# Low pieces of weights: from a GpSimd subtraction to a ScalarE copy and an adding transfer

## The chip, the cores and the metric

The kernel runs on one core of a Trainium2 chip. The metric is the device time of one execution in microseconds, shown as the median of several runs of the same program. The times of the profile are microseconds from the first instruction of one profiled execution. PE is TensorE (its weight loads are PEld), DVE is VectorE, ACT is ScalarE, POOL is GpSimd and SP is the queue that issues most loads.

## The reference, cut to what matters

The program is a two-layer backbone over 256 tokens of 2048 channels: an even layer (a convolution and a state-space layer in parallel), an odd layer (a gated MLP over chunks), each followed by a convolutional feed-forward part. What matters here is that nearly all of the work is products of activations with large float32 weights:

```python
proj = hn @ w_in                       # even mixer, 2048 x 3584
out = concat([y_conv, y_ssm]) @ w_out  # 2048 x 2048
z = gelu(hn @ w_in)                    # odd mixer, 2048 x 4096
...
z = hn @ w_in                          # feed-forward, 2048 x 8192, twice
return (a * silu(g)) @ w_out           # 4096 x 2048, twice
```

Beside them stand the modulation vectors, `silu(c) @ ada_w[layer]`, which read 2048 x 12288 weights for each layer.

## The kernel before

A product of float32 precision is made from products of a rounded type, float32r: both operands are cut into a high piece (the value rounded to float32r) and a low piece (the value less its high piece), and `mm3` adds three products, high by high (L137), high by low weights (L138) and low by high weights (L139), into one bank of PSUM.

`groups` goes through the weights in slabs of [128, 2048] float32 (1 MB): it loads a slab into a buffer `raw` (four of them, L157, on SP's queue), and for each half of it calls `split`, which fills a pair of buffers `hi` and `lo` (three of each, 128 x 1024); then come the 12 products of that half (two k tiles, two blocks of 128 tokens, three products of 512 columns each). In what follows one such half, with its 12 products, is called a split. There are 568 of them.

In `split` ACT writes `hi` as a copy of the half of `raw` (L130), and then POOL or DVE writes `lo` as `raw` less `hi` (L132 and L133). Which of them does it, `pool_every` sets: POOL takes every fourth or third split, or none, in parts of the even layer, and every second one from the end of the even mixer on (`PE5`, L1331). From there on splits come in pairs, one whose `lo` DVE makes and one whose `lo` POOL makes. A split can only begin when its buffers are free, and as there are three, that is when PE has finished the split three places ahead of it.

The order of the instructions on each engine comes from a scheduler that follows the order of the program and the priorities: loads and splits are written under `high_priority` (L156 and L161), `AHEAD2` places early. Each engine and each queue works strictly in its order.

Beside this, DVE does the 3x3 convolutions of the feed-forward part (`conv9`, L1249), the sums of the modulation vectors of the second layer (`ada_items_v`: slabs `rawa` of 512 KB, two buffers, loaded at L242 and multiplied and added into `adacc` at L244), the residual adds and the low pieces of the activations. PE does part of the modulation products of the first layer (L202), transposes (L1233, L390) and the rest. POOL's only other DMAs are five small loads at the start and while the state-space layer is built, among them `bc_in` (L617).

Of the kernel before, what the change touches and what calls it, by code (L numbers as in the profile page):

```python
# [8 lines left out]
F32 = mybir.dt.float32  # L9
# [49 lines left out]
class Builder:  # L59
# [68 lines left out]
    def split(self, hi, lo, raw):  # L128
        nc = self.nc
        nc.scalar.activation(hi, raw, AF.Copy)  # L130
        self.split_n += 1
        eng = nc.gpsimd if self.split_n % self.pool_every == 0 else nc.vector  # L132
        eng.tensor_sub(lo, raw, hi.bitcast(F32))  # L133
# [7 lines left out]
    def groups(self, wap, gs, toks, qs, ada=(0.0, 0.0), rate=None, crate=0.0, width=2, order=None, hold=0,  # L141
               hfs=(0, 1)):
        """ps[g][t] = x_t @ W[:, 512 g : 512 g + 512]; qs: (slab, first k tile of x)."""
# [81 lines left out]
    def ada_items_v(self, l, v):  # L225
        """the same with the products of the slabs on the vector engine, summed over partitions at the end."""
# [41 lines left out]
    def ada_pump(self, n, k=0):  # L268
        """n slabs' worth of the queue of products on the tensor engine (k = 0) or the vector engine (k = 1)."""
        q = self.ada_q[k]  # L270
        self.ada_credit[k] = min(self.ada_credit[k] + n, max(n, 4.0))
        while q and self.ada_credit[k] >= q[0][0]:
            c, f = q[0]
            q.pop(0)
            f()
            self.ada_credit[k] -= c
# [10 lines left out]
    def gate_row(self, l, v):  # L287
        """row form of a gate vector on every partition."""
        self.ada_until(self.ada_row, (l, v))
        row = self.hp.tile([128, D], F32, name="grow", tag="grow")  # L290
        for j in range(4):
            self.nc.sync.dma_start(row[:, 512 * j:512 * j + 512],
                                   self.ada_row[l, v][j:j + 1].to_broadcast([128, 512]))
        return row

    def mod_vecs(self, l, which, s=0):
        """(norm_g * (1 + scale), shift) with channels on partitions."""
# [28 lines left out]
    def ssq_rms(self, ssq, n, tag):  # L326
        """ssq [128, t, parts] -> 1/rms per token; the columns' chains are interleaved."""
# [38 lines left out]
    def norm_chunk(self, k0, nk, rows, r, gs, sh, xh, xl):  # L366
        """nk k tiles from k0 of the modulated rows, transposed and split."""
# [16 lines left out]
    def transposed(self, z, b):  # L384
        """PSUM [128 ch, 2, 256 tok]: channel tiles b, b + 1 of the token-major pair z."""
# [69 lines left out]
    def ada0_items(self, k0, nk):  # L455
        """shift and scale of the first mixer for both streams, nk k tiles from k0: quadrants hold the
        scale's even and odd k tiles, then the shift's."""
# [126 lines left out]
    def s5_powers(self):  # L584
        """ab^e (e = 1 .. 3) and f ab^k (k = 0 .. 4), channels (re, im)."""
# [24 lines left out]
    def s5_compact(self, T, p):  # L610
        """closures: powers of ab times C f and B for four pairs, both directions."""
# [25 lines left out]
    def s5_input(self, u):  # L637
        """u [128 tok (i, chunk), 4 (ctx, ctx, lat, lat), 512] -> X[(i, 32 ch), pair, chunk]."""
# [14 lines left out]
    def s5_tables(self, T, d, t, k):  # L653
        """cos and sin of the angle per chunk for four pairs."""
# [13 lines left out]
    def s5_group(self, T, d, sp):  # L668
        """closures for four pairs of state groups in one direction."""
# [138 lines left out]
    def s5_gelu(self, T):  # L808
        """closure: gelu of 128 channels of the readout, channels on partitions."""
# [16 lines left out]
    def s5_output(self, mh, ml):  # L826
        """gate of the readout, split into the last four k tiles."""
# [15 lines left out]
    def conv31(self, cts):  # L843
        """closures: 31 taps over some z tiles."""
# [15 lines left out]
    def conv31_pe(self, cts):  # L860
        """closures: the same by products with diagonal matrices of the taps."""
# [221 lines left out]
    # LayerNorm over channels on partitions.  # L1083
    def ln_items(self, zpp):
# [9 lines left out]
        def total(ps):  # L1094
            """the quadrants' sums (each on 32 partitions) added up, on every partition."""
# [125 lines left out]
    def conv9(self, z, ct, dst):  # L1221
        """closures: transposes of two 128-channel tiles of z and their 3x3 grid convolutions into dst."""
# [35 lines left out]
    def ffn(self, l, h, ssq, ada, ada_out):  # L1258
# [4 lines left out]
        with self.tc.tile_pool(name=f"fp{l}", bufs=1) as fp:  # L1263
# [7 lines left out]
            def half(g, gi):  # L1271
                """closures after the product of column group g (gi: pair)."""
# [92 lines left out]
def tile_w(w):  # L1365
    """[K, N] -> [N/512, K/512, 128, 4 * 512]"""
    K, N = w.shape
    return w.reshape(K // 512, 4, 128, N // 512, 512).transpose(3, 0, 2, 1, 4).reshape(N // 512, K // 512, 128, 2048)


def chan(v):
    """[..., n * 128] -> [128, ..., n]"""
# [4 lines left out]
def layout(i):  # L1377
# [31 lines left out]
    def state(v):  # L1409
        """[2, 32, 64, 16] -> [4 T, (2 g, 64), 2 d, 4 q, 16]"""  # L1410
# [34 lines left out]
```

## Time and profile before

| | us |
|---|---|
| median of 3 runs | 2123.08 |
| lowest and highest of them | 2120.01, 2129.16 |
| profiled execution (its span, first to last instruction) | 2123.7 |
| PE busy | 1960.5 |
| DVE busy | 1697.2 |
| ACT busy | 984.5 |
| POOL busy | 794.8 |

The profile gives the profiled execution's time as its span; nothing beside it is listed. A busy engine is one that has an instruction under way; matmuls overlap, so PE can show as busy while it is not at its fastest. The chain of work that ended last is followed back from the last instruction through whatever released each step. A stretch of the timeline shows starts and durations, so that an end is the sum of the two.

### The profile page before, as it was taken

What the parts mean: (1) busy time and instruction counts of PE and PEld (TensorE: products, weight loads), DVE (VectorE), ACT (ScalarE), POOL (GpSimd) and SP (SyncE); (2) the same over time, 40 slices, a digit from 0 to 9 for tenths busy, and PEclk for the clock granted to TensorE, in tenths of its full rate; (3) what the DMA queues carried; (4) which work ended last, traced back from release to release, by engine and by line L of the source; (5) the groups of instructions that cost most, each with busy time, mean ns of one, the idle gap of its engine ahead of it and who ended that gap; (6) DMA issues with size and microseconds to landing.
All of it is one profiled execution on the core that took longest, in us unless ns stands there. A gap on an engine that the chain in (4) does not pass through costs nothing.

```text
span 2123.7 us, 26033 instructions
## 1 busy us (share of the span) xinstructions
PE 1960.5 (92%) x9384; PEld 1500.1 (71%) x9384; DVE 1697.2 (80%) x2806; ACT 984.5 (46%) x1407; POOL 794.8 (37%) x384
## 2 busy tenths in 40 slices
PE   5999999899899999999999789899899989999997
PEld 2566566686677776778777567777677867888886
DVE  5469998977778997789999776976789997368874
ACT  3354344663455543345454354343455543355553
POOL 4312203511033444445445244443433443444443
PEclk8999999899999999999999899999999999999999
DMA  9985766444866677787667777767765576555552
GB/s 380 394 345 220 265 251 258 169 174 185 311 250 255 237 274 260 280 291 249 223 235 274 265 256 284 269 252 290 265 238 211 195 246 239 181 192 184 182 203 110
DMA packets 91645, 522.47 MB, mean 246 GB/s; under 512 B 11334, under 2 KB 11590, under 8 KB 41974
## 3 DMA queue, kind: packets, MB, share of 16 engines
q1 hardware_dynamic: 88684, 517.09, 66.3%
q10 hardware_dynamic: 2448, 2.57, 0.4%
q8 instruction: 73, 1.20, 0.2%
q0 software_dynamic: 384, 1.16, 0.1%
q14 instruction: 56, 0.46, 0.1%
HBM read 518.65 MB, written 2.13 MB: 245 GB/s over the span
## 4 chain that ended last, share of the span: by engine, by line
PE 30%; DVE 21%; issue 7%; DMA 7%; POOL 3%; ACT 1%; SPq 0%; ACTq 0%; DVEq 0%; POOLq 0%
PE mm L137 10%; PE mm L138 9%; PE mm L139 9%; DVE adacc L244 7%; DMA rawa<-in_ada_w 6%; DVE lo L133 5%; POOL lo L133 3%; DVE ca L1249 3%; DVE cg L1249 3%; PE tp L1233 1%; DVE ca L1299 1%; DVE al L1301 1%; ACT hi L130 0%; DVE h L411 0%; DVE wk L410 0%
## 5 line engine op out<-in xcount | busy, mean ns | idle before, releaser
L133 POOL TENSOR_TENSOR lo<-raw,hi 128x1024 fp32r<-128x1024 f32 x258 | 693.7, 2689 | 1201.0 <-ACT hi L130 1115.9
L130 ACT ACTIVATE hi<-raw 128x1024 fp32r<-128x1024 f32 x568 | 599.1, 1059 | 773.6 <-PE mm L139 612.0
L138 PE MATMUL mm<-lo,xh 128*128 128x512 f32 x1632 | 649.8, 398 | 41.9 <-DVE lo L133 41.0
L137 PE MATMUL mm<-hi,xh 128*128 128x512 f32 x1632 | 656.9, 404 | 3.5 <-DVE acc L993 1.9
L139 PE MATMUL mm<-hi,xl 128*128 128x512 f32 x1632 | 646.2, 397 | 3.0 <-DVE xl L1136 1.7
L133 DVE TENSOR_TENSOR lo<-raw,hi 128x1024 fp32r<-128x1024 f32 x310 | 422.4, 1365 | 154.9 <-ACT hi L130 154.4
L244 DVE SCALAR_TENSOR_TENSOR adacc<-rawa,cst,adacc 128x1024 f32<-128x1024 f32 x192 | 336.1, 1757 | 101.2 <-DMA rawa<-in_ada_w 98.1
L138 PEld LDWEIGHTS mm<-lo,xh 128*128 128x128 f32 x1632 | 311.5, 191 | 115.9 <-DVE lo L133 53.3
L137 PEld LDWEIGHTS mm<-hi,xh 128*128 128x128 f32 x1632 | 311.0, 191 | 108.1 <-issue 31.7
L139 PEld LDWEIGHTS mm<-hi,xl 128*128 128x128 f32 x1632 | 310.5, 190 | 72.2 <-DVE xl L1136 3.3
L138 PE MATMUL mm<-lo,ah 128*128 128x512 f32 x640 | 258.8, 404 | 13.8 <-DVE lo L133 13.1
L137 PE MATMUL mm<-hi,ah 128*128 128x512 f32 x640 | 257.8, 403 | 0.0
L139 PE MATMUL mm<-hi,al 128*128 128x512 f32 x640 | 257.0, 402 | 0.0
L1249 DVE SCALAR_TENSOR_TENSOR ca<-tp,fcw,ca 128x189 f32<-128x189 f32 (+2 forms) x512 | 179.6, 418 | 12.6 <-ACT ca L1236 12.6
L1249 DVE SCALAR_TENSOR_TENSOR cg<-tp,fcw,cg 128x189 f32<-128x189 f32 (+2 forms) x512 | 179.9, 418 | 9.1 <-ACT cg L1236 9.1
L138 PEld LDWEIGHTS mm<-lo,ah 128*128 128x128 f32 x640 | 122.7, 192 | 48.1 <-DVE lo L133 17.2
L137 PEld LDWEIGHTS mm<-hi,ah 128*128 128x128 f32 x640 | 122.7, 192 | 32.1 <-issue 2.5
L139 PEld LDWEIGHTS mm<-hi,al 128*128 128x128 f32 x640 | 122.8, 192 | 31.4 <-issue 2.5
L856 DVE SCALAR_TENSOR_TENSOR zc<-zpad,ecw,zc 128x256 f32<-128x256 f32 x300 | 139.1, 530 | 0.0
L202 PE MATMUL ad<-raw,cst 128*32 128x512 f32 x512 | 79.4, 621 | 3.6 <-DVE wk L210 2.7
L390 PE MATMUL tp<-ident,wk 128*128 128x128 f32 x184 | 34.3, 314 | 29.9 <-DVE wk L376 16.7
L411 DVE TENSOR_TENSOR h<-h,wk 128x512 f32<-128x512 f32 x56 | 57.4, 1034 | 1.1
(279 smaller groups left out, 1519.0 us busy)
## 6 DMA issues: line engine op xcount, KB each, us to landing
raw<-in_f_w_in SPq DMA_DIRECT2D x128, 1024.0 KB, 4.8
rawa<-in_ada_w SPq DMA_DIRECT2D x192, 512.0 KB, 5.2
raw<-in_ada_w SPq DMA_DIRECT2D x84, 1024.0 KB, 6.1
raw<-in_f_w_out SPq DMA_DIRECT2D x64, 1024.0 KB, 4.8
raw<-in_o_w_in SPq DMA_DIRECT2D x32, 1024.0 KB, 6.8
raw<-in_e_w_in SPq DMA_DIRECT2D x28, 1024.0 KB, 7.0
raw<-in_e_w_out SPq DMA_DIRECT2D x16, 1024.0 KB, 6.9
raw<-in_o_w_out SPq DMA_DIRECT2D x16, 1024.0 KB, 6.9
```

The lines of the kernel that those rows point to most:

```text
L130: nc.scalar.activation(hi, raw, AF.Copy)
L133: eng.tensor_sub(lo, raw, hi.bitcast(F32))
L137: nc.tensor.matmul(ps, xh, wh, start=first, stop=False)
L138: nc.tensor.matmul(ps, xh, wl, start=False, stop=False)
L139: nc.tensor.matmul(ps, xl, wh, start=False, stop=last)
L202: nc.tensor.matmul(st["ps"][32 * j:32 * j + 32, :], self.cst[:, kt], raw[:, 512 * j:512 * j + 512], start=kt == 0, stop=kt == KT - 1, tile ...
L244: nc.vector.scalar_tensor_tensor(a, raw, self.cst[:, kt, 0:1], a, op0=OP.mult, op1=OP.add)
L390: self.nc.tensor.transpose(tp[:, a * 256 + t * 128:a * 256 + t * 128 + 128], z[t][:, c0:c0 + 128], self.ident)
L411: nc.vector.tensor_add(h[:, t, c], h[:, t, c], m)
L856: nc.vector.scalar_tensor_tensor(o, src, w, o, op0=OP.mult, op1=OP.add)
L1233: nc.tensor.transpose(tp[:, a * 256 + t * 128:a * 256 + t * 128 + 128], z[t][:, c0 + 128 * a:c0 + 128 * a + 128], self.ident)
L1249: nc.vector.scalar_tensor_tensor(oo, s[:, y0 + dy:y1 + dy, x0 + dx:x1 + dx], w, oo, op0=OP.mult, op1=OP.add)
```

## The change

For the splits that were POOL's, `lo` is made in two steps: ACT writes the negated, rounded half of `raw` into `lo`, and a DMA issued from POOL's queue adds `raw` to it in place, from SBUF to SBUF. DVE's splits stay as they are. All else in the diff is comments and blank lines that went, which moves the lines that follow by five.

```diff
     def split(self, hi, lo, raw):
         nc = self.nc
         nc.scalar.activation(hi, raw, AF.Copy)
         self.split_n += 1
-        eng = nc.gpsimd if self.split_n % self.pool_every == 0 else nc.vector
-        eng.tensor_sub(lo, raw, hi.bitcast(F32))
+        if self.split_n % self.pool_every:
+            nc.vector.tensor_sub(lo, raw, hi.bitcast(F32))
+        else:
+            nc.scalar.activation(lo, raw, AF.Copy, scale=-1.0)
+            nc.gpsimd.dma_start(lo.bitcast(F32), raw, accum_op=OP.add)
```

The scheduler's order on ACT, in the second feed-forward part, where two column groups of its first product are copied out of PSUM (`z`). Two slabs stand here; of each, the first half is DVE's and the second was POOL's. Before:

```order
L130 ACTIVATE hi_15089<-raw_15087 128x1024
L130 ACTIVATE hi_15114<-raw_15087 128x1024
L1278 ACTIVATE z_15079<-mm_14895 128x512
L130 ACTIVATE hi_15138<-raw_15136 128x1024
L1278 ACTIVATE z_15081<-mm_14896 128x512
L130 ACTIVATE hi_15160<-raw_15136 128x1024
```

And with the change (L132 is the copy to `hi`, L137 the negated copy to `lo`):

```order
L132 ACTIVATE hi_15315<-raw_15313 128x1024
L137 ACTIVATE lo_15341<-raw_15313 128x1024
L132 ACTIVATE hi_15340<-raw_15313 128x1024
L1283 ACTIVATE z_15305<-mm_15117 128x512
L132 ACTIVATE hi_15365<-raw_15363 128x1024
L1283 ACTIVATE z_15307<-mm_15118 128x512
L137 ACTIVATE lo_15388<-raw_15363 128x1024
L132 ACTIVATE hi_15387<-raw_15363 128x1024
```

The negated copy has come in as one more instruction for every slab, and it stands ahead of the copy to `hi` of its own split, although the program writes it behind.

POOL's order from the end of the even layer to the end of the program, before:

```order
L133 TENSOR_TENSOR lo<-raw,hi 128x1024 x39
L232 MEMSET adacc 128x2048
L133 TENSOR_TENSOR lo<-raw,hi 128x1024 x30
L232 MEMSET adacc 128x2048
L133 TENSOR_TENSOR lo<-raw,hi 128x1024 x28
```

And with the change:

```order
L138 DMA lo<-raw 128x1024 x39
L237 MEMSET adacc 128x2048
L138 DMA lo<-raw 128x1024 x30
L237 MEMSET adacc 128x2048
L138 DMA lo<-raw 128x1024 x29
```

Each subtraction has become an issue of a DMA in the same place; the clearing of `adacc` stays between them, one place later in the last case.

## Rows read from the trace of the kernel before

**Rows 1.** The page, busy time of each engine, share of the span, instructions.

```profile
PE 1960.5 (92%) x9384; PEld 1500.1 (71%) x9384; DVE 1697.2 (80%) x2806; ACT 984.5 (46%) x1407; POOL 794.8 (37%) x384
```

**Rows 2.** The page, chain that ended last: shares by engine, then by line.

```profile
PE 30%; DVE 21%; issue 7%; DMA 7%; POOL 3%; ACT 1%; SPq 0%; ACTq 0%; DVEq 0%; POOLq 0%
PE mm L137 10%; PE mm L138 9%; PE mm L139 9%; DVE adacc L244 7%; DMA rawa<-in_ada_w 6%; DVE lo L133 5%; POOL lo L133 3%; DVE ca L1249 3%; DVE cg L1249 3%; PE tp L1233 1%; DVE ca L1299 1%; DVE al L1301 1%; ACT hi L130 0%; DVE h L411 0%; DVE wk L410 0%
```

**Rows 3.** Three stretches, all instructions.

```profile
core 0: us, PE busy (x) PEld busy (x) DVE busy (x) ACT busy (x) POOL busy (x), PEclk, DMA share, GB/s
0.00:100.00 100.00, 75.23 (x372) 40.15 (x376) 51.84 (x180) 36.94 (x63) 43.83 (x64) 0.91 0.96 385
600.00:1600.00 1000.00, 922.35 (x4037) 727.18 (x4037) 830.14 (x1100) 449.32 (x566) 426.19 (x157) 0.97 0.73 262
1600.00:2123.00 523.00, 499.01 (x2216) 403.97 (x2215) 397.36 (x715) 253.44 (x316) 214.66 (x86) 0.99 0.54 193
```

**Rows 4.** The same stretches, low pieces (L133) alone: DVE, POOL, clock, DMA.

```profile
600.00:1600.00 1000.00, 218.67 (x152) 417.21 (x152) 0.97 0.73 262
1600.00:2123.00 523.00, 110.89 (x87) 214.66 (x86) 0.99 0.54 193
```

**Rows 5.** Timeline of PE, 1920 to 1927: start, duration, instruction.

```profile
1920.35 0.39 PE L138 MATMUL mm<-lo,xh 128*128 128x512 f32 x1
1920.58 0.39 PE L139 MATMUL mm<-hi,xl 128*128 128x512 f32 x1
1920.81 0.60 PE L1233 MATMUL tp<-ident,z 128*128 128x128 f32 x4
...
1926.73 0.39 PE L137 MATMUL mm<-hi,xh 128*128 128x512 f32 x1
1926.96 0.39 PE L138 MATMUL mm<-lo,xh 128*128 128x512 f32 x1
```

**Rows 6.** Timelines of ACT and POOL, the split that belongs to these.

```profile
1921.01 1.06 ACT L130 ACTIVATE hi<-raw 128x1024 fp32r<-128x1024 f32 x1 [1.61 <-PE mm L139]
1922.14 2.41 POOL L133 TENSOR_TENSOR lo<-raw,hi 128x1024 fp32r<-128x1024 f32 x1 [2.97 <-ACT hi L130]
```

**Rows 7.** Who waited for whom: us in total, times, longest.

```profile
POOL lo L133 <- ACT hi L130: 1115.9, 244, 36.8
ACT hi L130 <- PE mm L139: 612.0, 369, 7.2
DVE adacc L244 <- DMA rawa<-in_ada_w: 98.1, 52, 5.6
PE mm L138 <- DVE lo L133: 54.0, 34, 2.9
```

**Rows 8.** The page, groups: busy us, mean ns | idle before, releaser.

```profile
L133 POOL TENSOR_TENSOR lo<-raw,hi 128x1024 fp32r<-128x1024 f32 x258 | 693.7, 2689 | 1201.0 <-ACT hi L130 1115.9
L133 DVE TENSOR_TENSOR lo<-raw,hi 128x1024 fp32r<-128x1024 f32 x310 | 422.4, 1365 | 154.9 <-ACT hi L130 154.4
L244 DVE SCALAR_TENSOR_TENSOR adacc<-rawa,cst,adacc 128x1024 f32<-128x1024 f32 x192 | 336.1, 1757 | 101.2 <-DMA rawa<-in_ada_w 98.1
```

**Rows 9.** The same instructions by line or tile: ns least/median/most.

```profile
L130 ACT ACTIVATE hi<-raw x568: 1040/1061/1079, 35.7 to 2102.7; 128x1024 fp32r<-128x1024 f32 x190
L133 DVE TENSOR_TENSOR lo<-raw,hi x310: 1199/1218/3415, 38.4 to 2101.1; 128x1024 fp32r<-128x1024 f32 x155
L244 DVE SCALAR_TENSOR_TENSOR adacc<-rawa,cst,adacc x192: 1216/1282/3449, 547.0 to 1767.7; 128x1024 f32<-128x1024 f32 x192
```

**Rows 10.** Line L617, POOL's loads of 256 KB: issue in ns, then landing.

```profile
L617 POOL DMA_DIRECT2D bc_in<-in_s_bc x4: 536/578/585, 2.5 to 374.4; - x4
...
DMA to landing us min/median/max: 3.0/6.6/8.2
```

**Rows 11.** Tile rawa, SP's loads of 512 KB: issue in ns, then landing.

```profile
L242 SPq DMA_DIRECT2D rawa<-in_ada_w x192: 327/328/664, 539.8 to 1761.8; - x192
...
DMA to landing us min/median/max: 3.5/5.2/8.2
```

**Rows 12.** Line L157, SP's loads of weights, 1 MB each: from issue to landing.

```profile
DMA to landing us min/median/max: 4.6/5.0/13.6
```

## The prediction

> **What bounds the kernel now.** I read the busy times first [rows 1]: PE has work in 92% of the span, DVE in 80%, ACT in 46% and POOL in 37%, so PE is the engine that the rest must feed, and DVE the one that may fail to. The chain that ended last [rows 2] agrees: 30% of the span is PE's, 21% DVE's, 7% DMA (nearly all of it the loads of `rawa`) and 3% POOL's. I then cut the span where POOL makes every second low piece [rows 3, 4]. From 600 to 1600 POOL makes 152, so a pair of splits takes 1000/152 = 6.58 us, with DVE busy for 83% and the 16 DMA engines for 73%. From 1600 to 2123 it makes 86, 6.08 us a pair, with PE busy for 95% and the DMA engines for 54%. Last I followed one of POOL's splits through the timelines [rows 5, 6]. PE's last product of the split three places ahead begins at 1920.58 and ends at 1920.97; ACT starts `hi` at 1921.01 and POOL starts `lo` at 1922.14, 0.07 us behind the end of `hi`. `lo` is there at 1924.55, and PE first needs it at 1926.96: 2.41 us to spare. PE's products are 0.23 us apart, so the two splits between keep it busy until then. POOL's subtraction is thus off PE's path. What it costs shows on DVE: the same instructions whose median is 1218 and 1282 ns have means of 1365 and 1757 ns [rows 8, 9], and PE waits for DVE's low pieces for 54.0 us in all [rows 7].
>
> **The change, part by part.** *Removed:* 258 subtractions of 2689 ns on POOL, 694 us [rows 8]. They lie beside PE's work, so their own time gives nothing. If they are what stretches DVE's instructions, DVE gets back (1365 - 1218) x 310 = 46 us and (1757 - 1282) x 192 = 91 us.
>
> *Added on ACT:* 258 negated copies. The same copy to `hi` takes 1061 ns [rows 9], so 274 us, and ACT goes from 46% to 59%. Its cover is the 612 us in which ACT waits for PE to free a buffer [rows 7]. The copy now stands ahead of `hi` of its own split, which it delays by about 0.8 us: `hi` would end near 1922.9 and is needed at 1926.73 [rows 5]. I cost this at nothing. Were the cover gone, `hi` would be late next, by under 1.1 us a pair.
>
> *Added on POOL:* 258 issues at 0.58 us [rows 10], 150 us in place of 694. Behind an issue on POOL stand only later issues and six clearings of `adacc`, so nobody waits for POOL itself.
>
> *The new chain to `lo`.* The buffer is free when the last product that reads `lo` ends, 1920.35 + 0.39 = 1920.74 [rows 5]. With the hand-overs of today, 0.04 and 0.07 us, and 1.06 us for the copy, the transfer is issued at 1921.91. It may take 1926.96 - 1921.91 = 5.05 us before PE waits.
>
> *The transfer's price* no row shows. At the start the engines move 385 GB/s at a share of 0.96 [rows 3], so 401 GB/s when all are busy: 512 KB take 1.31 us, 256 KB take 0.65. POOL's quickest 256 KB took 3.0 us from issue to landing [rows 10], so 2.35 us are not data. An adding transfer must read `raw` and also `lo`, and write `lo`: one pass of 1.31 us if the second read is free, two passes if both reads go through the engine in turn, three if the write does too. Alone that is 3.7, 5.0 or 6.3 us to landing. Loads beside it add something: SP's 1 MB loads have a median 0.4 us over their quickest [rows 12], its 512 KB loads 1.7 us [rows 11]; between these I take 1.0. The bounds are 3.7 us below and 8.2 us, POOL's slowest 256 KB, above. I take two passes under load, 6.0 us, since two reads for one write is what the instruction names. The Trainium skill (Collectives: The Full Stack, "The bandwidth ceiling: the fold count and why AG ≠ RS ≠ AR") says that an add in the DMA engines costs nothing by itself but halves the rate, because two sources are read through one ring; by it the value is two passes too, and no run here shows it yet.
>
> *What 6.0 us does where PE sets the pace.* It is 0.95 us over the 5.05. With three buffers a transfer is released by the end of the pair before the last one; when it is late, two periods hold one undelayed pair and one chain, so each pair grows by half of the lateness, 0.48 us. From 1600 on: 86 x 0.48 = **+41 us**. Before 600, 258 - 152 - 86 = 20 transfers: **+5** (at most 10).
>
> *What it does where the DMA engines are full.* From 600 to 1600 a pair needs 0.73 x 6.58 = 4.80 us of the engines. Two passes add 2.62: 7.42 us a pair where 6.58 were taken. If the engines set the pace, that is 0.84 x 152 = **+128 us**. It would show as `rawa` landing later, whose waits are already 98.1 us and on the path [rows 2, 7], and as late adding transfers. The chain's own lateness is smaller there (pairs are longer) and not counted again.
>
> *Relief of DVE.* Where transfers set the pace, a faster DVE only waits. I count half of the 54.0 us that PE waits for DVE's low pieces: **-25**.
>
> Sum: 41 + 5 + 128 - 25 = +149 us. The profiled execution's span is 2123.7, 0.6 over the median of the runs shown, 2123.08, so the sum goes against either alike: **2273 us**.
>
> **The rivals.**
> *One pass: faster (0.27).* If the second read hides behind the first, the engines need 4.80 + 1.31 = 6.11 us a pair, under 6.58, and the transfer lands in 3.7 + 0.4 to 3.7 + 1.0 = 4.1 to 4.7 us, under 5.05. Then no wait is new and DVE's 137 us come back. What PE waits for it, 54.0 us, is the price: 2070 us. For it: DVE's `adacc` is 7% and its `lo` 5% of the chain [rows 2]. Against it: the two reads. The point at which it decides is a landing in 5.05 us. A rule of the Trainium skill speaks for it (DMA: Bandwidth & Descriptors, "Anatomy of one DMA — SWDGE (gpsimd) path"): about 2.0 us plus the bytes at 436 GB/s, an estimate of 3.2 us here; by it the time is this rival's. The trace agrees with that only at its quickest; its medians are 5.2 and 6.6 us [rows 10, 11].
>
> *Three passes: much slower (0.10).* 3.93 us of the engines: 4.80 + 3.93 = 8.73 from 600 to 1600, +2.15 x 152 = +327; later 0.54 x 6.08 + 3.93 = 7.21, +1.13 x 86 = +97. 2548 us. For it: nothing in the trace shows an adding transfer at all. Against it: reads and writes of a plain load go through at one price.
>
> *Two passes that fit: no change (0.11).* Weights are loaded four buffers ahead and the modulation sums are not due until their layer, so the loads may give way: then the 128 us fall away, and 41 + 5 against 25 to 54 of relief leave 2115 to 2145, some 2130.
>
> **How the numbers follow.** My forecast has 0.52, with its own range 2150 to 2450: the upper end is a surcharge of 1.7 us in place of 1.0 and no relief, (0.83 x 86 = 71) + 10 + 128 = +209, and a landing near 8.2 us, with half of a lateness of 3.15 us on 238 pairs, for which I allow up to 2450. Faster than all is the rival with one pass, 2045 to 2110. The range reaches over both, 2045 to 2450, and leaves out three passes and the tails. A measurement here can tell about 0.5%, 10.6 us. Faster by more: 0.27; within it: 0.11; slower: 0.52 + 0.10 = 0.62.
>
> **What would show it.** Right: the page of the kernel after has PE waiting at the products with `lo` for the adding transfer, for over 100 us in all; these transfers land in 5.5 to 7 us; the DMA share from 600 on is over 0.9; DVE's `lo` and `adacc` have means within 5% of their medians; ACT is busy for some 1260 us and POOL for some 250. Wrong: landings under 5 us with no wait of PE (then one pass); a DMA share that rises by 0.2 and not 0.4; DVE's means as long as before, which would say that POOL's subtractions did not stretch them; or the negated copies late on ACT, which would put the wait there.

## The result, and the profile after

The changed kernel takes 2506.01 us (median of 4 runs, 2501.43 to 2510.68) against 2126.12 us for the kernel before in the same comparison: a ratio of 1.179, interval 1.176 to 1.183. The forecast had the sign and the place right and the size wrong: +149 us were forecast, about +380 us measured, outside the range. The profiled execution has a span of 2505.6 us against 2123.7, so its difference is 381.9 us.

The page of the kernel after, busy times, then the chain that ended last by engine, then two of its queues and groups (columns as in [rows 1, 2, 8]; a queue line is packets, MB, share of 16 engines' span):

```profile
PE 2085.4 (83%) x9384; PEld 1564.3 (62%) x9384; DVE 1475.2 (59%) x2806; ACT 1220.4 (49%) x1665; POOL 327.0 (13%) x384
...
q1 hardware_dynamic: 88684, 517.09, 55.9%
q0 software_dynamic: 37536, 136.45, 29.3%
...
issue 60%; PE 19%; DMA 10%; POOL 5%; DVE 4%; ACT 2%; POOLq 0%; ACTq 0%; DVEq 0%; SPq 0%
...
L143 PE MATMUL mm<-lo,xh 128*128 128x512 f32 x1632 | 689.6, 423 | 229.8 <-DMA lo<-raw 226.4
L135 DVE TENSOR_TENSOR lo<-raw,hi 128x1024 fp32r<-128x1024 f32 x310 | 381.0, 1232 | 616.9 <-ACT hi L132 615.8
L138 POOL DMA_DIRECT2D lo<-raw x258 | 224.8, 871 | 2050.9 <-ACT lo L137 1667.4
L137 ACT ACTIVATE lo<-raw 128x1024 fp32r<-128x1024 f32 x258 | 273.0, 1058 | 294.6 <-PE mm L143 288.2
L249 DVE SCALAR_TENSOR_TENSOR adacc<-rawa,cst,adacc 128x1024 f32<-128x1024 f32 x192 | 244.1, 1280 | 179.7 <-DMA rawa<-in_ada_w 179.3
```

PE is busy for 83% of the span, not 92% [rows 1], and PE now sits idle before the low products (L143), waiting for the adding transfer. Of the chain, 60% is "issue", time for which the profile shows no wait, so the chain says little here, and the waits below are read instead. DVE's two groups have means close to the medians of before, 1232 and 1280 ns [rows 8, 9]: what stretched them is gone, and neg_pool_add below shows that it was POOL's arithmetic. The transfers' own queue (q0) takes 29.3% of the engines' time: 0.293 x 2505.6 / 258 = 2.85 us of all 16 engines for each 512 KB.

Who waited for whom in the kernel after (us in total, times, longest), then SP's own queue:

```profile
DVE lo L135 <- ACT hi L132: 615.8, 202, 10.7
ACT hi L132 <- issue: 447.1, 119, 9.6
PEld mm L143 <- DMA lo<-raw: 407.7, 142, 6.6
PE mm L143 <- DMA lo<-raw: 350.3, 124, 6.2
...
DVE adacc L249 <- DMA rawa<-in_ada_w: 179.3, 77, 6.1
...
PE mm L143 <- DVE lo L135: 2.8, 5, 0.9
```

```profile
SPq L162 <- DMA lo<-raw: 1333.0, 231, 16.2
```

PE waits for the adding transfer in 124 of the 258 cases, 350.3 us in all, 2.83 us each. Its wait for DVE's low pieces fell from 54.0 to 2.8 us [rows 7]. The wait for `rawa` went from 98.1 to 179.3 us [rows 7]. SP's loads now wait for transfers to let go of `raw`, but ACT's waits for loads stay small: the largest such row of the kernel after is 81.9 us, for the even layer's first weights, and the rows for the feed-forward weights are under 4 us. The 447.1 us of ACT's `hi` for which the profile shows no releaser are not loads either: 117 of these 119 copies start within 0.3 us of the end of the PE product that reads their buffer last, so they wait for PE.

Three stretches follow, cut at the PE products that end the first feed-forward part's 192 splits, the odd layer's 96 and the second feed-forward part's 192 (96, 48 and 96 pairs); columns as in [rows 3]; the first line of the kernel before begins 4 us into its part. First the kernel before, then the kernel after:

```profile
590.00:1205.00 615.00, 575.20 (x2552) 449.41 (x2550) 542.40 (x784) 281.48 (x352) 267.50 (x99) 0.99 0.71 257
1205.00:1532.00 327.00, 295.78 (x1266) 236.86 (x1268) 240.48 (x253) 136.40 (x169) 134.38 (x50) 0.95 0.76 272
1532.00:2111.00 579.00, 558.97 (x2484) 451.56 (x2476) 446.99 (x761) 287.95 (x365) 242.26 (x97) 0.99 0.56 198
```

```profile
586.00:1370.00 784.00, 631.43 (x2561) 483.28 (x2560) 453.09 (x790) 373.06 (x452) 88.67 (x99) 0.91 0.91 269
1370.00:1777.00 407.00, 319.04 (x1264) 248.93 (x1268) 195.39 (x254) 181.65 (x218) 44.12 (x50) 0.90 0.92 279
1777.00:2493.00 716.00, 606.64 (x2484) 475.57 (x2484) 390.06 (x761) 374.73 (x460) 84.50 (x96) 0.93 0.83 231
```

Measured between those products, the parts went from 619 to 784, from 326 to 407 and from 579 to 716 us: +165, +81 and +137; what comes before them stays at 586. The granted clock falls in each part. Summed over the program it stands at its lower level, 1.2 GHz, for 126 us before and for 365 us after.

One late transfer shows both losses. The timeline of PE in the kernel after (start, duration, instruction, idle before and what ended it), and POOL's issue of that transfer:

```profile
2306.38 0.39 PE L144 MATMUL mm<-hi,xl 128*128 128x512 f32 x1
2306.60 0.39 PE L142 MATMUL mm<-hi,xh 128*128 128x512 f32 x1
2310.51 0.80 PE L143 MATMUL mm<-lo,xh 128*128 128x512 f32 x1 [3.52 <-DMA lo<-raw]
2311.10 0.63 PE L144 MATMUL mm<-hi,xl 128*128 128x512 f32 x1
2311.53 0.63 PE L142 MATMUL mm<-hi,xh 128*128 128x512 f32 x1
...
2313.23 0.58 PE L143 MATMUL mm<-lo,xh 128*128 128x512 f32 x1
2313.64 0.40 PE L144 MATMUL mm<-hi,xl 128*128 128x512 f32 x1
2313.89 0.40 PE L142 MATMUL mm<-hi,xh 128*128 128x512 f32 x1
2314.12 0.39 PE L143 MATMUL mm<-lo,xh 128*128 128x512 f32 x1
```

```profile
2301.88 0.87 POOL L138 DMA_DIRECT2D lo<-raw  x1 [4.57 <-ACT lo L137]
```

The transfer is issued at 2301.88 and PE has its result some 8.6 us later. PE stands for 3.52 us. The products after the wait begin 0.43 us apart instead of 0.23 until 2313.6; from 2310.5 on the profile has the granted clock at 0.50, which is 1.2 GHz, and from 2313.7 on at 1.00. So this wait is paid twice: once as idle time, and once in the products behind it.

### The profile page after: what moved, and what is told of

It is laid out like the page before. It is cut to its first block, busy times and chain, and to the rows that moved or that the text cites. A ratio compares the mean times of both kernels' runs of the same rounds, so it can differ in the third digit from the quotient of the medians.

```text
span 2505.6 us, 26728 instructions
## 1 busy us (share of the span) xinstructions
PE 2085.4 (83%) x9384; PEld 1564.3 (62%) x9384; DVE 1475.2 (59%) x2806; ACT 1220.4 (49%) x1665; POOL 327.0 (13%) x384
## 3 DMA queue, kind: packets, MB, share of 16 engines
q0 software_dynamic: 37536, 136.45, 29.3%
## 4 chain that ended last, share of the span: by engine, by line
issue 60%; PE 19%; DMA 10%; POOL 5%; DVE 4%; ACT 2%; POOLq 0%; ACTq 0%; DVEq 0%; SPq 0%
DMA lo<-raw 6%; POOL lo L138 5%; PE mm L143 5%; PE mm L144 4%; PE mm L142 4%; DMA raw<-in_e_w_in 2%; PE ad L207 2%; PE ad L480 1%; DMA raw<-in_ada_w 1%; PE ms L726 1%; PE tp L395 1%; DVE lo L135 1%; PE mm L881 1%; DVE w L774 0%; ACT hi L132 0%
## 5 line engine op out<-in xcount | busy, mean ns | idle before, releaser
L132 ACT ACTIVATE hi<-raw 128x1024 fp32r<-128x1024 f32 x568 | 595.3, 1051 | 678.5 <-issue 447.1
L143 PE MATMUL mm<-lo,xh 128*128 128x512 f32 x1632 | 689.6, 423 | 229.8 <-DMA lo<-raw 226.4
L135 DVE TENSOR_TENSOR lo<-raw,hi 128x1024 fp32r<-128x1024 f32 x310 | 381.0, 1232 | 616.9 <-ACT hi L132 615.8
L142 PE MATMUL mm<-hi,xh 128*128 128x512 f32 x1632 | 677.1, 418 | 3.0 <-ACT xh L1140 1.6
L144 PE MATMUL mm<-hi,xl 128*128 128x512 f32 x1632 | 673.4, 413 | 0.4 <-DVE xl L1141 0.4
L143 PEld LDWEIGHTS mm<-lo,xh 128*128 128x128 f32 x1632 | 328.9, 202 | 337.0 <-DMA lo<-raw 264.2
L138 POOL DMA_DIRECT2D lo<-raw x258 | 224.8, 871 | 2050.9 <-ACT lo L137 1667.4
L137 ACT ACTIVATE lo<-raw 128x1024 fp32r<-128x1024 f32 x258 | 273.0, 1058 | 294.6 <-PE mm L143 288.2
L143 PE MATMUL mm<-lo,ah 128*128 128x512 f32 x640 | 275.5, 430 | 123.9 <-DMA lo<-raw 123.9
L144 PEld LDWEIGHTS mm<-hi,xl 128*128 128x128 f32 x1632 | 328.6, 201 | 71.5 <-DVE lo L135 1.7
L249 DVE SCALAR_TENSOR_TENSOR adacc<-rawa,cst,adacc 128x1024 f32<-128x1024 f32 x192 | 244.1, 1280 | 179.7 <-DMA rawa<-in_ada_w 179.3
L143 PEld LDWEIGHTS mm<-lo,ah 128*128 128x128 f32 x640 | 130.5, 204 | 173.2 <-DMA lo<-raw 143.5
L415 DVE TENSOR_TENSOR wk<-mm,grow 128x512 f32<-128x512 f32 x56 | 38.1, 688 | 42.9 <-PE mm L144 42.9
```

The lines of the kernel that those rows point to most:

```text
L135: nc.vector.tensor_sub(lo, raw, hi.bitcast(F32))
L137: nc.scalar.activation(lo, raw, AF.Copy, scale=-1.0)
L138: nc.gpsimd.dma_start(lo.bitcast(F32), raw, accum_op=OP.add)
L142: nc.tensor.matmul(ps, xh, wh, start=first, stop=False)
L143: nc.tensor.matmul(ps, xh, wl, start=False, stop=False)
L144: nc.tensor.matmul(ps, xl, wh, start=False, stop=last)
```

## The experiments

The medians, and the parts of each profiled execution (us, cut as above: up to the first feed-forward part, that part, the odd layer, the second feed-forward part). Every ratio is to the kernel before on the same chip; that kernel's median was 2136.1 us beside neg_only, plain_copy, after_lo_last and after_f4, and between 2123.9 and 2126.7 beside the others. fill6 has added products and was not cut.

| kernel | median | ratio, interval | start | FF 1 | odd | FF 2 |
|---|---|---|---|---|---|---|
| before | 2126.1 | | 586 | 619 | 326 | 579 |
| after | 2506.0 | 1.176 to 1.183 | 586 | 784 | 407 | 716 |
| neg_only | 2005.6 | 0.926 to 0.950 | 560 | 577 | 298 | 561 |
| tiny_transfer | 2135.7 | 1.003 to 1.008 | 567 | 641 | 344 | 578 |
| plain_copy | 2304.1 | 1.066 to 1.090 | 576 | 697 | 379 | 637 |
| neg_pool_add | 2111.6 | 0.989 to 0.995 | 581 | 607 | 336 | 578 |
| before_dve | 2130.9 | 1.001 to 1.005 | 588 | 616 | 315 | 596 |
| after_pe4 | 2321.7 | 1.086 to 1.099 | 589 | 715 | 379 | 623 |
| fill6 | 2575.4 | 1.204 to 1.220 | | | | |
| after_no_rawa | 2382.4 | 1.116 to 1.129 | 594 | 709 | 366 | 693 |
| before_no_rawa | 2136.2 | 1.003 to 1.008 | 591 | 625 | 331 | 578 |
| after_lo_last | 2395.0 | 1.107 to 1.134 | 579 | 738 | 390 | 677 |
| after_f4 | 2372.8 | 1.097 to 1.123 | 586 | 724 | 410 | 643 |
| after_f4_last | 2296.6 | 1.077 to 1.086 | 579 | 690 | 392 | 617 |
| before_lo_last | 2109.8 | 0.990 to 0.995 | 585 | 607 | 317 | 578 |
| before_f4_last | 2108.4 | 0.989 to 0.995 | 586 | 610 | 315 | 583 |
| neg_add_last | 2091.5 | 0.981 to 0.987 | 576 | 603 | 317 | 577 |

### A ladder from no transfer to the adding one

**neg_only** leaves the transfer out:

```diff
             nc.scalar.activation(lo, raw, AF.Copy, scale=-1.0)
-            nc.gpsimd.dma_start(lo.bitcast(F32), raw, accum_op=OP.add)
```

> The transfers are left out: lo holds the negated high piece alone, so the output is not the reference's. POOL's subtractions are gone and ACT's 258 copies stay. If all of the loss comes from the transfer, this is at or below the kernel before: 2040 to 2110 us, with PE's wait for DVE's low pieces under the 54 us of before and DVE's means at their medians. If ACT's extra copies cost something by themselves, it is over 2140 us.

**plain_copy** makes the same transfer without the add, one read and one write:

```diff
-            nc.gpsimd.dma_start(lo.bitcast(F32), raw, accum_op=OP.add)
+            nc.gpsimd.dma_start(lo.bitcast(F32), raw)
```

> The transfer copies raw into lo and adds nothing (output not the reference's): one read for one write, the same chain, issue and hand-overs. Packets of 4 KB should take 160 ns where the adding ones take 328. If the data phase of the transfer and its load on the engines make the loss, landings fall from a mean of 6.8 to some 5.2 us, the DMA share to about 0.75, and the time to 2150 to 2250 us. If issue, hand-over or the fact of a POOL transfer make it, landings stay over 6 us and the time over 2400 us.

**tiny_transfer** adds only 16 of the 1024 columns, 8 KB in place of 512:

```diff
-            nc.gpsimd.dma_start(lo.bitcast(F32), raw, accum_op=OP.add)
+            nc.gpsimd.dma_start(lo[:, :16].bitcast(F32), raw[:, :16], accum_op=OP.add)
```

> The transfer adds 16 of the 1024 columns (64 bytes a partition) and the rest of lo stays the negated high piece, so the output is not the reference's. ACT's copies, POOL's issues, the hand-overs and the waits are all there; the data phase is not. If data and load make the loss, landings are 2 to 3 us and the time is that of neg_only within 1%: 2000 to 2030 us. If issue, hand-over and completion make a good part of it, 2060 us or more.

**neg_pool_add** keeps ACT's copy and lets POOL do the add:

```diff
-            nc.gpsimd.dma_start(lo.bitcast(F32), raw, accum_op=OP.add)
+            nc.gpsimd.tensor_add(lo, raw, lo.bitcast(F32))
```

> ACT's negated copy stays and POOL adds raw to it, so no transfer: ACT's part of the change with POOL's old work. The low piece is ready no later than before. If ACT's copies cost nothing, 2100 to 2140 us, DVE's adacc at a mean near 1.75 us again; all that neg_only gained would then be POOL's contention with DVE and none of it the missing wait for a low piece. If ACT's copies do cost, over 2150 us.

*Measured.* The medians go 2006, 2136, 2304, 2506: with the kernel before at 2126, the way to +380 us is some -120 for POOL's subtraction gone, +130 for a transfer with next to no data, +168 for one pass of 512 KB and +202 for the second pass and what else the add brings. The steps are good to some 25 us: neg_only and plain_copy ran beside a slower kernel before, and by the ratios the same steps are about -131, +143, +154 and +216. The step from tiny_transfer to plain_copy is not data alone, as the issue gets 0.34 us shorter in it. neg_only came out below what was expected (2040 to 2110), and plain_copy between its two theories: its landings fell as the first had it, to a mean of 5.3 us, but its time lies above that theory's 2150 to 2250. Issue, landing and queue in the three kernels with a transfer (issue in ns least/median/most; landing in us from issue; packets, MB, share), plain_copy first, then tiny_transfer, then the kernel after:

```profile
L138 POOL DMA_DIRECT2D lo<-raw x258: 527/527/577, 115.6 to 2281.8; - x129
...
DMA to landing us min/median/max: 2.8/5.1/10.7
...
q0 software_dynamic: 37536, 136.45, 15.5%
```

```profile
L138 POOL DMA_DIRECT2D lo<-raw x258: 860/869/1024, 116.5 to 2123.6; - x129
...
DMA to landing us min/median/max: 2.1/3.9/8.2
...
q0 software_dynamic: 37536, 3.29, 3.5%
```

```profile
L138 POOL DMA_DIRECT2D lo<-raw x258: 860/869/1160, 116.1 to 2485.6; - x129
...
DMA to landing us min/median/max: 4.5/6.4/11.6
```

The plain transfer takes 0.155 x 2301.7 / 258 = 1.38 us of the engines, the adding one 2.85: twice as much, so two passes is the right price, as the forecast took it. That it is the second read that fills the second pass, and not the add itself, no run separates. The issue of an adding transfer is 0.87 us long with 8 KB as with 512, 0.34 us over that of a plain one. The quickest landings are 2.1, 2.8 and 4.5 us; the medians lie 1.8 to 2.3 us above, and the slowest 6 to 8. The 8 KB transfer is there in 2.1 us at its quickest, yet its mean in the first feed-forward part, where the engines are 74% busy, is 4.6 us. The trace shows that this is waiting beside other transfers: the 23 that have the engines nearly free of other queues (under 10% busy in the 2 us behind the issue) land after 2.2 us on average, the 98 that find them over 90% busy after 4.7.

tiny_transfer misses what the theory of data expected: some 130 us over neg_only come with next to no data. They are on PE's path for `lo`:

```profile
PE mm L143 <- DMA lo<-raw: 101.0, 71, 3.7
```

A kernel's two losses can be added up and set against neg_only, which has neither subtraction nor transfer: PE's wait for the transfers, and the excess of slow-paced products, those that begin 0.30 to 0.52 us after the one before them in place of 0.227. For tiny_transfer, plain_copy and the kernel after the sums are 101 + 28 = 129, 210 + 65 = 275 and 350 + 119 = 469 us, where the spans lie 134, 293 and 496 us over neg_only's. So these two make up about 95% of what any of the transfers costs. The hold of a transfer on `raw` is not among them: ACT's `hi` waits 184.5 us without a shown releaser in tiny_transfer, 75.1 in neg_only, but there too 91 of the 93 copies start within 0.3 us of the end of the PE product that frees their buffer. How the 129 us divide into issue and queueing was not separated.

DVE's two groups in neg_only, then in neg_pool_add (mean ns is the second number):

```profile
L135 DVE TENSOR_TENSOR lo<-raw,hi 128x1024 fp32r<-128x1024 f32 x310 | 380.0, 1228 | 212.2 <-ACT hi L132 210.3
...
L248 DVE SCALAR_TENSOR_TENSOR adacc<-rawa,cst,adacc 128x1024 f32<-128x1024 f32 x192 | 244.9, 1280 | 130.2 <-DMA rawa<-in_ada_w 128.2 <-DMA adacc<-in_ada_r 1.6
```

```profile
L135 DVE TENSOR_TENSOR lo<-raw,hi 128x1024 fp32r<-128x1024 f32 x310 | 418.3, 1352 | 154.5 <-ACT hi L132 74.8 <-POOL lo L138 56.9 <-issue 21.3
L249 DVE SCALAR_TENSOR_TENSOR adacc<-rawa,cst,adacc 128x1024 f32<-128x1024 f32 x192 | 326.9, 1709 | 109.8 <-DMA rawa<-in_ada_w 106.8 <-DMA adacc<-in_ada_r 2.8
```

With POOL's arithmetic back, the longer means are back, 1352 and 1709 ns, close to those before [rows 8]. neg_pool_add has all of ACT's 258 copies and is a little under the kernel before, so the copies cost nothing that shows, as forecast. Its time is in the range that was expected for this.

### How much each late transfer costs

**after_pe4** gives POOL's place every fourth split instead of every second from the end of the even mixer on, which takes 120 of the 258 transfers away; the others go to DVE. **before_dve** is its base, the kernel before with those low pieces all on DVE (18 subtractions stay on POOL):

```diff
-PE5 = 2
+PE5 = 4
```

> One transfer for four splits from the end of the even mixer on: 120 in place of 240, the other low pieces on DVE, which is idle for 40% of the time. The engines get half of the added load, so their share stays under 0.85 and landings near 5.5 us. If both lateness and load come from the transfers, at least half of the 382 us goes: 2130 to 2300 us. If what hurts is the fixed part of each chain alone, each transfer is late by about 1.5 us and pays it in full: 120 x 1.5 over the 2010 us of neg_only, near 2190 us, with the clock on top.

> The kernel before with all low pieces from the end of the even mixer on made by DVE, so neither POOL nor a transfer. DVE gets 240 x 1.22 = 293 us more and loses the stretch of some 220 us. If DVE's contention with POOL cost more than the help it gave, this is at or under 2123 us: 2060 to 2120. If DVE is then the bound, 2150 us or more.

*Measured.* before_dve is 0.3% above the kernel before, between its two theories: DVE alone can carry all low pieces with hardly a loss. after_pe4 keeps 138 transfers and stands 2321.7 - 2130.9 = 191 us above this base, 1.38 us for each. That is past the top of what was expected. The engines are less loaded here (landing median 5.7 us). A late transfer has no late neighbour to share its lateness with, so by the forecast's rule it costs the whole 0.95 us and not half of it; 1.38 is still more.

**fill6** puts six more high products, which have their operands, ahead of a split whose `lo` a transfer makes, to tell idle time from the clock:

```diff
+                    if self.split_n % self.pool_every == 0 and (qi or hf != hfs[0]):
+                        for _ in range(FILL):
+                            nc.tensor.matmul(ps[g][0], tq[0][0][:, k0 + hf * 2, tq[0][2]], hi[:, 0],
+                                             start=False, stop=False)
```

> Six products that are not needed (high piece by the same activations, added once more, so the output is not the reference's) stand ahead of the 12 products of every transfer's split that does not open a bank: 6 x 0.23 = 1.4 us of work for PE where it otherwise waits 2.8 us in half of these splits and not at all in the rest. If idle time lowers the granted clock and the lower clock costs time, the mean clock rises from 0.928 to over 0.95, products at half speed become fewer, and the time stays within 60 us of 2506 although PE does 320 us more. If the clock has no part in it, the splits that did not wait pay for the added products: 2570 us or more, at an unchanged share of low clock.

*Measured.* Span and granted clock, the kernel after, then fill6:

```profile
core 0: 2505.6 us, clock 0.928
```

```profile
core 0: 2567.6 us, clock 0.974
```

The clock is back at the level of the kernel before (0.971), and the time at 1.2 GHz falls from 365 to 134 us. The excess of slow-paced products falls from 149 to 66 us, and PE's wait for transfers from 350.3 to 125.8. So it is idle PE that lowered the clock. The time still rises, by 69 us, over the 60 that this theory allowed (its rival had 2570 us or more, but at an unchanged clock): the 1542 added products take 350 us at 0.227 us each, more than the 308 that the two falls give back.

### Loads beside the transfers

**after_no_rawa** loads two slabs `rawa` and uses them again in place of the other 190 loads; **before_no_rawa** is the same edit to the kernel before:

```diff
-                raw = self.yp.tile([128, 1024], F32, name="rawa", tag="rawa", bufs=2)
-                nc.sync.dma_start(raw, self.A["ada_w"][l, v, kt, :, c])
+                if len(self.rawa) < 2:
+                    raw = self.yp.tile([128, 1024], F32, name=f"rawa{len(self.rawa)}")
+                    nc.sync.dma_start(raw, self.A["ada_w"][l, v, kt, :, c])
+                    self.rawa.append(raw)
+                raw = self.rawa[i % 2]
```

> The changed kernel without 190 of the 192 loads of modulation weights (the two first slabs are used over again, so the output is not the reference's): 95 MB less for the DMA engines, 250 us of their time, all of it in the first feed-forward part and the odd mixer. If full engines carry the loss there, the first feed-forward part goes from 8.2 to under 7.5 us a pair while the second one stays at 7.4, and the distance to before_no_rawa is under 330 us. If it is the lateness of each chain alone, the distance stays near 380 us.

> The kernel before without the same loads, as the control: DVE's waits for rawa (98 us) go, some of them on the path. 2060 to 2110 us on every theory.

*Measured.* The distance between the two is 2382.4 - 2136.2 = 246 us, in place of 380. So these loads carry about a third of the loss, and two thirds are there without them. In the first feed-forward part the distance is 709 - 625 = 84 us in place of 165, and 709 us are 7.39 a pair, as expected. Not all of the loads lie in that part and the odd layer: 30 of the 192 are issued later, and the second feed-forward part goes from 137 to 115 us. The control missed: without these loads the kernel before is 0.5% slower, not faster, though its DVE waited 98.1 us for them and the chain named them [rows 2, 7]. That wait was DVE's alone: PE's wait for DVE's low pieces is 57.1 us without the loads, 54.0 with them. Why the time rises was not found.

### More room

**after_lo_last** writes the negated copy ahead of `hi` and puts each split's four low products behind its eight high ones, so that `lo` is needed later (in the scheduler's order `hi` then comes first all the same, in 238 of the 240 later splits with a transfer); **before_lo_last** does the second part to the kernel before:

```diff
-                            self.mm3(ps[g][i], xh[:, kt, tsl], xl[:, kt, tsl], hi[:, a], lo[:, a],
...
+                            nc.tensor.matmul(ps[g][i], xh[:, kt, tsl], hi[:, a], start=st_ and a == 0, stop=False)
+                            nc.tensor.matmul(ps[g][i], xl[:, kt, tsl], hi[:, a], start=False, stop=False)
+                    for i, (xh, xl, tsl) in enumerate(tq):
+                        for a in range(2):
+                            kt = k0 + hf * 2 + a
+                            nc.tensor.matmul(ps[g][i], xh[:, kt, tsl], lo[:, a], start=False, stop=en_ and a == 1)
```

> Each split's eight products with hi come first and its four with lo last, so lo is needed 1.6 us later; the transfers are untouched. ACT takes hi before the negated copy, which gives 0.4 us back. If the lateness of lo on PE (the chain of three buffers) sets the pace, each pair gains about half of 1.2 us and some of TensorE's clock: 2290 to 2380 us. If full DMA engines set it, the time stays over 2460 us.

> The kernel before with each split's products with lo last: nothing of the change in it, the same arithmetic in another order. PE waits for DVE's low pieces for 54 us in the kernel before; with 1.8 us more to spare most of that goes: 2060 to 2110 us. If these waits only move to the next instruction, no change (2110 to 2140).

**after_f4** gives the two feed-forward parts a fourth buffer for `lo`, with the negated copy ahead of `hi`:

```diff
-                    lo = self.wp.tile([128, 2, 512], F32R, name="lo", tag="lo", bufs=3)
+                    if self.ep and self.split_n % 4 == 3:
+                        lo = self.ep.tile([128, 2, 512], F32R, name="lo", tag="lo", bufs=1)
+                    else:
+                        lo = self.wp.tile([128, 2, 512], F32R, name="lo", tag="lo", bufs=3)
```

> A fourth lo buffer in the two feed-forward parts (192 of the 240 later transfers), so a transfer there can start a split, about 2.7 us, earlier. The transfers' bytes stay. If the chain sets the pace, the waits of PE for lo nearly vanish in those parts and the time is 2150 to 2250 us. If the DMA engines are what is full, the first feed-forward part (with the modulation loads) keeps over 7.4 us a pair and the time is 2290 us or more.

**after_f4_last** and **before_f4_last** have both of these edits:

> The changed kernel with both remedies at once: in the two feed-forward parts a fourth buffer for lo (every fourth split), everywhere the negated copy ahead of hi, and each split's 8 products with hi ahead of its 4 with lo. Theory (lateness on top of full DMA engines): an adding transfer now has some 5.5 us more room than in the change, so in the feed-forward parts hardly one is late, and these parts fall to what the DMA engines need: the first to 7.4 us a pair, 96 pairs, 715 us (784 in the change, 724 with the fourth buffer alone, 738 with the order alone); the second to 6.2 us a pair, 600 us (716, 643, 677). The odd layer, which has no fourth buffer, stays at the order's 390. Start 582 and the tail 13: 2300 in all, PE waiting for adding transfers under 120 us. Rival (room doesn't help beyond what one remedy gave, since the transfers queue behind one another and behind the loads): 2360 to 2400, PE's wait above 200 us.

> The kernel before with the same two remedies, as the control. The low piece of GpSimd has 2.4 us to spare already, so a fourth buffer and products with lo last take away only PE's 54 us of waiting for low pieces: 2090 to 2130 (2110 with the order alone). Rival (more room lets the DVE work that is behind catch up further): under 2080.

*Measured.* Each remedy gives back over 100 us, both together 209 us (2296.6). after_lo_last is 15 us above what the theory of the chain expected. after_f4 came out as the theory of full engines had it: 2372.8 us, and 724/96 = 7.54 us a pair in the first feed-forward part, at a DMA share of 0.97. The odd layer has no fourth buffer and serves as control: after_f4 leaves it at 410. The three stretches of after_f4_last, and PE's wait:

```profile
578.00:1268.00 690.00, 600.36 (x2562) 460.00 (x2561) 450.28 (x790) 376.13 (x453) 88.14 (x98) 0.96 0.99 304
1268.00:1660.00 392.00, 319.14 (x1262) 250.32 (x1261) 193.47 (x253) 183.56 (x220) 44.19 (x50) 0.90 0.96 290
1660.00:2277.00 617.00, 571.96 (x2485) 450.87 (x2484) 389.15 (x761) 376.56 (x459) 84.02 (x96) 0.98 0.96 268
```

```profile
PE mm L184 <- DMA lo<-raw: 136.5, 77, 4.7
```

In the feed-forward parts the engines are now full or nearly so, 99% and 96%, and PE's wait there is down to 38.0 and 22.5 us: what is left is close to the engines' own floor, 690/96 = 7.19 and 617/96 = 6.43 us a pair. The theory that full engines are left when lateness goes forecast 2300; its rival had 2360 to 2400. (PE's wait in all was to be under 120 us; nearly half of the 136.5 is the odd layer's.) The landing grew, to a median of 8.5 us, and did no more harm. The same edits to the kernel before give under 1%, 2108.4 us, and before_lo_last, 2109.8, is at the edge between its two theories.

**neg_add_last** is neg_pool_add with the low products last, no transfer at all:

> The negated copy on ScalarE with GpSimd adding raw to it in place, no adding transfer, and each split's products with lo last: the two variants that came out a little under the kernel before, 2112 and 2110, in one. If both take away the same waits of PE for low pieces: 2095 to 2115. If they are separate: 2085 to 2095. Rival (ScalarE's copies become late when both are there): above 2125.

*Measured.* 2091.5 us, ratio 0.984 (0.981 to 0.987): faster than both kernels, and the fastest of all that compute the whole reference. It lies where separate gains were expected (2085 to 2095); since neg_pool_add and before_lo_last alone give 0.8% and 0.7%, the two gains add.

## Why the prediction was wrong in size

**Direction and place: right, and shown.** The adding transfer takes two passes (2.85 against 1.38 us of the engines for a plain one; 2.62 forecast). It lands at a median of 6.4 us (5.5 to 7 forecast), PE waits for it for 350 us (over 100 forecast), and DVE's means fall to their medians. The DMA share was to be over 0.9 from 600 on; it is 0.91 and 0.92, but 0.83 in the second feed-forward part. ACT is busy for 1220 us (1260 forecast) and POOL for 327 (250), as the issue is 0.87 us and not 0.58.

**The step that failed: "What 6.0 us does where PE sets the pace"**, +41 us, of which the second feed-forward part shows the plain case: +137 us there, 137/96 = 1.43 us a pair in place of 0.48. The rule of the step holds; three things that went into it were too small or left out. (Of the 233 us that the forecast lacked, some 96 are here, 118 in the next step and 25 in the relief of DVE.)

- *The room and the landing.* The issue starts 0.29 us behind the end of ACT's copy, in place of the 0.07 us taken from POOL's subtraction [rows 6], which leaves 5.05 - 0.22 = 4.83 us. The mean landing in this part is 6.3 us: half of 1.47 would be 0.73 us a pair.
- *The spread.* I computed with one landing time. They run from 4.5 to 11 us in this part; a late one is paid, and an early one gives nothing back. PE waited 44 times for 104.7 us: every second pair or so, as the rule of one undelayed pair between two late ones has it, but 2.38 us each time, 1.09 us a pair. The spread is what the waits lacked: put the part's 95 measured landings one after another through the same rule (each wait is the landing less 4.83 us of room, less the wait of the pair before), and it gives 44 waits and 1.11 us a pair, an estimate from the trace; with their mean in place of each it gives 0.74.
- *The clock*, which the forecast did not consider. The excess of slow-paced products in this part went from 7 to 44 us, 0.39 us a pair. Over the whole kernel it went from 47 to 149 us, 102 of the 382 us; 91 of the 102 fall in times at which the profile has the clock at 1.2 GHz. With the waits this makes 1.09 + 0.39 = 1.48, near the 1.43 measured.

**The step "What it does where the DMA engines are full"**, +128 us: the floor was about right and the sum wrong. The engines' time for a pair in the first feed-forward part is 0.91 x 784 / 96 = 7.43 us; 7.42 were forecast. But they were not full at that: a pair took 8.17 us at a share of 0.91. With room enough the part falls to 7.19 us a pair at 0.99 (after_f4_last), 71 us over the kernel before; the other 94 of its 165 us are lateness and clock. The sentence "the chain's own lateness is smaller there … and not counted again" is the error: lateness is larger there. PE's waits in the kernel after, first feed-forward part, odd layer, second feed-forward part:

```profile
PE mm L143 <- DMA lo<-raw: 152.5, 51, 6.2
PE mm L143 <- DMA lo<-raw: 78.9, 25, 5.8
PE mm L143 <- DMA lo<-raw: 104.7, 44, 6.0
```

That is 1.59, 1.64 and 1.09 us a pair. The loads act through the landings, whose means are 7.3, 7.1 and 6.3 us: the same rule, with each part's own landings and 4.83 us of room, gives an estimate of 1.66, 1.61 and 1.11. So in the kernel after late transfers set the pace in all three parts, and the engines' floor lies below it and comes out only with more room. In the first feed-forward part and the odd layer together +246 us came where +128 stood.

The second feed-forward part also meets that floor, which the forecast kept out of its sum: with room it stays at 617 us at a share of 0.96, over the 579 before. By the forecast's own terms it was close, 0.54 x 6.08 + 2.62 = 5.90 us of a pair's 6.08.

**The start**, +5: no difference, 586 us both times, but as a balance: neg_only has 560 there, and PE waits 14.3 us for transfers in the kernel after. **Relief of DVE**, -25: undersized. PE's wait for DVE's low pieces does go, from 54.0 to 2.8 us, and neg_only shows some 120 us with subtraction and transfer both gone; in the kernel after this relief lies hidden under the transfers, which cost 496 us against neg_only and not 382. **ACT's copies**, nothing: shown by neg_pool_add.

**The range.** Its upper end was set under its own sum: half of 3.15 us on 238 pairs is 375 us, which is 2499 and not 2450. That 2499 lies near the measured 2506 is luck: it took landings of 8.2 us on every pair, where the means were 6.3 to 7.3, and nothing for the clock.

**The rivals.** One pass, 2070 us: plain_copy is that rival, and it is 7.8% slower than the kernel before. Its engines' time is as that rival took it (1.38 us against 1.31), its landing not: a median of 5.1 us and a mean of 5.3 where 4.1 to 4.7 stood. The rule behind it (the Trainium skill, DMA: Bandwidth & Descriptors, "Anatomy of one DMA — SWDGE (gpsimd) path") gives an estimate of 3.2 us for 512 KB. The trace of plain_copy agrees where the engines are nearly free of other queues (a mean of 3.5 us, 56 transfers) and not under load (6.3 us where they are over 90% busy); the adding transfer never took under 4.5. The other rule cited from the Trainium skill (Collectives: The Full Stack, "The bandwidth ceiling: the fold count and why AG ≠ RS ≠ AR") is stated for the adds of a ReduceScatter: half the rate, because of two source reads. The 2.85 against 1.38 us agree with the half; its reason no run here shows. Three passes, 2548 us, comes nearest to the measured time by its number and is refuted as a mechanism by the same two figures. No change, 2130 us: the loads did not give way, as the first feed-forward part stays at 690 us against 619 even with room enough (after_f4_last).

## What to carry to other kernels

A transfer on the path is to be priced by the spread of its landings under load, not by one landing time: a late one is paid, and an early one gives nothing back. Ahead of moving arithmetic onto the DMA engines, add up the engines' time in every stretch, and take that as a floor only: here it was 7.2 to 7.4 us a pair, and late transfers made it 8.2. And look at the granted clock wherever a change gives PE new waits: here the slow products cost 102 us beside the 280 us that longer gaps between products did (406 to 686 us).

## What was not expected

- POOL's subtraction, off PE's path with 2.4 us to spare, cost the kernel before some 120 us (neg_only, ratio 0.926 to 0.950); yet moving nearly all of it to DVE gives nothing (before_dve, 1.003). How it reaches PE is shown only in part: PE's wait for DVE's low pieces is 54.0 us in the kernel before and 12.7 in neg_only.
- An adding transfer of 8 KB costs about as much as the subtraction of 512 KB that it replaces: 2135.7 against 2126 us. It needs 2.1 us at its quickest and 4.6 us on average among loads.
- The issue of an adding transfer holds POOL for 0.87 us, of a plain one for 0.53 us.
- Taking 190 loads of 512 KB out of the kernel before gained nothing (1.003 to 1.008), although the chain of waits had named them.
